# The context's output projection between the sample halves, the second matrix's sums two pairs late, and the spatial weights' low parts on VectorE

## The chip, the cores and the metric

The kernel runs on one core of one Trainium2 chip. The metric is device time in microseconds (us) for one execution. A core has TensorE (PE, matrix products; PEld is its weight loading), VectorE (DVE), ScalarE (ACT), GpSimd (POOL), and SyncE (SP), which here only issues DMAs. POOL and ACT issue DMAs too.

## The reference, cut

One layer of a diffusion backbone, applied to 1024 sample tokens and 256 context tokens (all float32, D = 1024, D_FF = 4096), with the same weights for both:

```
u   = rmsnorm(x, g1) * (1 + sc1) + sh1
xp, su, sv, q, k, v, o, gates, br = split(u @ w_in)
y_a = pool_branch(xp);  y_b = su * (w_sgu rmsnorm(sv) + b);  y_c = mlstm_branch(q, k, v, ...)
merged = sum_r sigmoid(br_r) * (y_r @ w_branch[r])
x   = x + gt1 * (merged @ w_out)                                  # output projection
u2  = rmsnorm(x, g2) * (1 + sc2) + sh2                            # modulation
x   = x + gt2 * (square(relu(u2 @ w_ff1)) @ w_ff2)                # feed-forward: first, second matrix
y   = rmsnorm(x, g_final)
```

The final states of the mLSTM for the context are outputs too.

## The kernel before

The 1280 rows are eight sample tiles of 128 rows (0 to 7, in groups 0 and 1 of 512 columns of the transposed data) and two context tiles (8 and 9, group 2). Every float32 product is made of three products of rounded parts: each operand is split into a high part (a cast, mostly on ACT) and a low part (raw minus high, mostly on DVE), and PE computes high x high, high x low, low x high. So every weight that is loaded costs a DMA, a cast and a subtraction ahead of PE. In the spatial projection (`sv`) the subtraction is on POOL (`eng=G`).

The stages by time: input, modulation and first projections to about 150 us; the mLSTM heads and the spatial values to 360; pooling and gating to 490; the gate products to 850; branch outputs to 1000; the output projection from about 1025; the feed-forward's first matrix from 1137 to 1549; its second matrix to the end.

The output projection `project_out(tiles, c0, n, weights)` makes `n` columns from `c0` on for each tile: 24 matmuls, then DVE multiplies by the gate and adds to the rows in `xt`, and ACT squares them for the norm (L1221 to L1224). Sample tiles take two halves of 512 columns, context tiles four quarters of 256 (`context_out(q)`, with weights of its own from `context_weights(q)`). `modulate_ff(g)` makes the norm of a group, the normalised rows (`xn`, half on ACT at L1184, half on DVE at L1186), transposes them on PE (`pt`, L1192), scales on ACT (L1201) and splits them.

The matrices of the feed-forward are multiplied by a scheme with seven products for a 2 x 2 block product (Strassen's, in Winograd's form), which needs sums of quarters. `quarter_sums` and `split_sum` (L824, L834) make T1 to T4 from the modulated rows. The first matrix is done in 16 pairs (`FeedPair`, fp 0 to 15) of 24.9 us: `begin` loads and splits raw weights (`a_..`, `s_..`), `contexts` does the context (`fc`), `rest` the products `fB` (with a quarter itself) and `fT` (with a sum), and `sums` makes from the four results, after relu and square, the second matrix's left operands: the results go to DRAM (`scr_h`, from ACT's queue), four sums on DVE (L1277 to L1280) go to `scr_s`, from POOL's queue. `second_sums(fp)` loads four quarters of the second matrix, has POOL make four differences in place (L1292) and stores them to `scr_t` (L1293).

The second matrix takes seven products in the order 1, 2, 6, 7, 4, 5, 3. For each of 16 fp a right operand (`r_`, from w_ff2 or `scr_t`) and a left one (`l_`, from `scr_h` or `scr_s`) is loaded by SP and split (L1352, L1353). PE multiplies them into the banks `w_0` to `w_3` (samples, 12 matmuls per fp); the context's rows (`c_`) go into `w_4`.

One SBUF buffer `z` holds 20 slots of 512 columns that are reused (`zs(i)`). In the feed-forward slots 0 to 3 and 4 to 7 hold raw weights of even and odd pairs, 12 to 15 and 8 to 11 the results of even and odd pairs, 16 to 19 the second matrix's quarters. The raw operands of the first ten fp of product 1 go into slots `FREE[fp]` and `FREE[fp] + 1`.

The order of instructions on each engine is set by a scheduler, which builds a timeline from the program's order and the free rooms. Where an engine is wrapped in `Pinned`, its instructions stay in the order in which the program writes them. An engine works through its queue in order, and so do the queues from which it issues DMAs.

Of the kernel before, what the change touches and what calls it, by code (L numbers as in the profile page):

```python
# [7 lines left out]
F32 = mybir.dt.float32  # L8
F32R = mybir.dt.float32r
AF = mybir.ActivationFunctionType  # L10
ALU = mybir.AluOpType
# [37 lines left out]
def hybrid_step(  # L49
# [39 lines left out]
    def load_w(src, name, raw=None, eng=V):  # L89
        raw = fetch_w(src, name) if raw is None else raw  # L90
        hi = wp.tile([P, 1024], F32R, tag="hi", name=f"hi_{name}", bufs=NHL)
        lo = wp.tile([P, 1024], F32R, tag="lo", name=f"lo_{name}", bufs=NHL)
        A.copy(hi, raw)
        eng.tensor_tensor(lo, raw, hi.bitcast(F32), ALU.subtract)
        return hi, lo
# [613 lines left out]
    vn = []  # L709
    vsq = cp.tile([P, NT, 2], F32, name="vsq")  # L710
    for q in range(2):
        wq = [load_w(w_sv[q, hf], f"sv{q}_{hf}", eng=G) for hf in range(2)]
        for i in range(NT):
            g, o = (i * P) // 512, (i * P) % 512
            if q == 0:
                vn.append(slot(f"vn{i}", F32))
            ps = ps_mm(f"sv{q}_{i}")
            for k in range(KT):
                whi, wlo = wq[k // 4]
                s = slice((k % 4) * 256, (k % 4 + 1) * 256)  # L720
                uh, ul = uT[k][g]
                PE.matmul(ps[:, :256], uh[:, o : o + P], whi[:, s], start=k == 0, stop=False)
                PE.matmul(ps[:, :256], ul[:, o : o + P], whi[:, s], start=False, stop=False)
                PE.matmul(ps[:, :256], uh[:, o : o + P], wlo[:, s], start=False, stop=k == KT - 1)
            A.copy(vn[i][:, q * 256 : (q + 1) * 256], ps[:, :256])
            A.activation(ps[:, 256:512], ps[:, :256], AF.Square, accum_out=vsq[:, i, q : q + 1])
# [6 lines left out]
    def zs(i, n=1):  # L733
        return z[:, i * 512 : (i + n) * 512]
# [185 lines left out]
    def load_half(src, name, view=lambda t: t):  # L920

        raw = first4(f"raw_{name}", F32)
        SP.dma_start(view(raw), src)
        hi, lo = six(f"hi_{name}"), ring(f"lo_{name}")
        A.copy(hi, raw)  # L925
        V.tensor_tensor(lo, raw, hi.bitcast(F32), ALU.subtract)
        return hi, lo
# [193 lines left out]
    def out_weights(hf, ks=range(KT)):  # L1121

        ws = []
        for k in ks:
            raw = tmp2(f"raw_wo{hf}_{k}")
            SP.dma_start(raw, w_out[hf, k])
            if hf == 0:
                rooms = (six, ring) if k < 6 else (first4, first4)
            else:
                rooms = (slot, slot) if k < 4 else (six, ring)  # L1130
            hi, lo = (room(f"{x}_wo{hf}_{k}") for room, x in zip(rooms, ("hi", "lo")))
            A.copy(hi, raw)
            V.tensor_tensor(lo, raw, hi.bitcast(F32), ALU.subtract)
            ws.append((hi, lo))
        return ws

    def context_weights(q):

        src = w_out[q // 2][:, :, q % 2 * 256 : q % 2 * 256 + 256].rearrange("(j k) p c -> j p k c", k=2)
        return [load_half(src[i], f"wc{q}_{i}", lambda t: t.rearrange("p (k c) -> p k c", k=2)) for i in range(4)]  # L1140

    w_out0 = out_weights(0)
    mT = [[] for _ in range(KT)]
# [24 lines left out]
    def modulate_ff(g):  # L1168
        t0, n = GROUPS[g]
        tiles = range(t0 // P, (t0 + n) // P)  # L1170
        fs = small([P, 4], f"fs{g}")[:, : len(tiles)]
        V.reduce_sum(fs, fsq[:, tiles[0] : tiles[-1] + 1, 0 : 4 if g == 2 else 2], axis=mybir.AxisListType.X)
        r = rstd_of(fs, len(tiles), f"f{g}")

        j = 1 if g == 2 else 0
        for qt in range(4):
            xn = []
            for ii, i in enumerate(tiles):
                if ii % 2 == 0:
                    t = tmp2(f"xn{i}_{qt}")  # L1180
                v = t[:, (ii % 2) * 256 : (ii % 2) * 256 + 256]
                xv = xt[i][:, qt * 256 : (qt + 1) * 256]
                if ii % 2 == 0:
                    A.activation(v, xv, AF.Copy, scale=r[:, ii : ii + 1])  # L1184
                else:
                    V.tensor_scalar(v, xv, r[:, ii : ii + 1], None, ALU.mult)  # L1186
                xn.append(v)
            for kk in range(2):
                k = qt * 2 + kk
                ps = ps_sd(f"pt2{g}_{k}")  # L1190
                for ii in range(n // P):
                    PE.transpose(ps[:, ii * P : (ii + 1) * P], xn[ii][:, kk * P : (kk + 1) * P], ident)  # L1192
                if g == 2:
                    c = slot(f"u2{k}c")
                    u2c[k] = hi, lo = c[:, 0:256], c[:, 256:512]
                    A.activation(ps[:, :n], ps[:, :n], AF.Identity, bias=sh2[:, k, j : j + 1], scale=a2[:, k, j : j + 1])
                    V.tensor_copy(hi, ps[:, :n])
                    V.tensor_tensor(lo, ps[:, :n], hi.bitcast(F32), ALU.subtract)
                    continue
                rf = raw2[g][k] = slot(f"u2r{k}_{g}", F32)  # L1200
                A.activation(rf, ps[:, :n], AF.Identity, bias=sh2[:, k, j : j + 1], scale=a2[:, k, j : j + 1])  # L1201
                if g == 0 or k >= 4:
                    hi, lo = slot(f"u2h{k}_{g}"), slot(f"u2l{k}_{g}")
                    V.tensor_copy(hi, rf)
                    V.tensor_tensor(lo, rf, hi.bitcast(F32), ALU.subtract)
                    u2s[f"B{1 + k // 4}{1 + g}", k % 4] = hi, lo

    def project_out(tiles, c0, n, weights):

        for i in tiles:  # L1210
            g = min(i // 4, 2)
            o = i * P - GROUPS[g][0]
            full = ps_mm(f"po{c0}_{i}")
            ps = full[:, :n]
            for k in range(KT):
                whi, wlo = weights(k)
                mh, ml = mT[k][g]
                PE.matmul(ps, mh[:, o : o + P], whi, start=k == 0, stop=False)
                PE.matmul(ps, ml[:, o : o + P], whi, start=False, stop=False)
                PE.matmul(ps, mh[:, o : o + P], wlo, start=False, stop=k == KT - 1)  # L1220
            V.tensor_tensor(ps, ps, gt1[(2 if g == 2 else 0) + c0 // 512][:, c0 % 512 : c0 % 512 + n], ALU.mult)  # L1221
            xc = xt[i][:, c0 : c0 + n]
            V.tensor_tensor(xc, xc, ps, ALU.add)  # L1223
            A.activation(ps, xc, AF.Square, accum_out=fsq[:, i, c0 // n : c0 // n + 1])  # L1224
            if c0 + n == D:
                SP.dma_start(scr_x[i], xt[i])

    def context_out(q):
        ws = context_weights(q)
        project_out((8, 9), q * 256, 256, lambda k: tuple(w[:, k % 2 * 256 : k % 2 * 256 + 256] for w in ws[k // 2]))  # L1230

    project_out(range(8), 0, 512, lambda k: w_out0[k])
    w_out1 = out_weights(1)
    project_out(range(5), 512, 512, lambda k: w_out1[k])
    modulate_ff(0)
    project_out(range(5, 8), 512, 512, lambda k: w_out1[k])
    context_out(0)
    context_out(1)  # L1240
    modulate_ff(1)
    quarters = (("B11", 0, 0), ("B21", 0, 4), ("B12", 1, 0), ("B22", 1, 4))
    raw2q = {nm: raw2[g][o : o + 4] for nm, g, o in quarters}
    context_out(2)
    context_out(3)

# [35 lines left out]

    def second_sums(fp):

        q = [zs(16 + i) for i in range(4)]
        for r in range(2):
            SP.dma_start(zs(16 + 2 * r, 2), w_ff2[2 * fp + r])
        b11, b12, b21, b22 = q  # L1290
        for out, x, y in ((b11, b12, b11), (b12, b22, b12), (b22, b22, b11), (b21, b22, b21)):
            G.tensor_tensor(out, x, y, ALU.subtract)  # L1292
        G.dma_start(scr_t[fp], zs(16, 4).rearrange("p (q c) -> p q c", c=512))  # L1293


    pairs = {}
# [1 line left out]
    def feed_pair(fp):  # L1298
        odd = fp % 2
        pairs[fp] = FeedPair(  # L1300
            f"{fp}", fp, (w_ff1[2 * fp], w_ff1[2 * fp + 1]), 4 if odd else 0, range(8, 12) if odd else range(12, 16), u2s, u2c)

    for fp in (0, 1):
        feed_pair(fp)
        pairs[fp].begin()
    modulate_ff(2)
    quarter_sums(raw2q)
    for nm in ("T4", "T3", "T2", "T1"):
        split_sum(u2s, raw2q, nm)
    for fp in (0, 1):  # L1310
        pairs[fp].contexts()
    for fp in range(NFP):
        if fp not in pairs:
            feed_pair(fp)
            pairs[fp].begin()
            pairs[fp].contexts()
        pairs[fp].rest()
        pairs[fp].sums()
        del pairs[fp]
        second_sums(fp)  # L1320


    pa.close()
# [21 lines left out]
    }  # L1345


    FREE = (0, 2, 16, 18, 12, 14, 4, 6, 8, 10)

    def split2(raw, room):  # L1350
        hi, lo = room("h"), room("l")
# [234 lines left out]
```

## Time and profile before

| | |
|---|---|
| median of 3 runs | 1937.88 us (1936.84 to 1939.31) |
| profiled execution | 1941.46 us |
| its span on the core | 1939.7 us |
| PE busy | 1905.1 us (98%) |
| DVE, ACT, POOL busy | 67%, 44%, 20% of the span |
| DMA | 318.56 MB, 164 GB/s over the span |

Times in the views are of the profiled execution, from the start of its span. A row of the timeline reads: start, duration, engine, line, operation, output<-inputs, shapes, count, and in brackets the idle time ahead of it with what ended it. A row of the waits reads: engine and what it waited with, what released it, us in all, times, longest. A row of DMA issues ends with the count, the size of one and the median time from issue to landing.

### The profile page before, as it was taken

The numbers are of one execution on the slowest core, as the hardware profiler recorded it, in microseconds if no ns is written. First come the engines' busy times: TensorE is split into PE (matmuls) and PEld (weight loads), VectorE is DVE, ScalarE is ACT, GpSimd is POOL, SyncE is SP. The second block draws the span as 40 slices with busy tenths as digits, with TensorE's granted clock in tenths as the row PEclk, the third lists the DMA queues.
The fourth block names the chain that finished last, engine by engine and source line by source line (L and its number), as shares of the span: only waits on it lengthen the run. The fifth ranks groups of instructions, "written<-read, shape, count | busy, mean of one in ns | idle before, by whom it ended". The sixth has DMA issues, their size and how long they took to land.

```text
span 1939.7 us, 28224 instructions
## 1 busy us (share of the span) xinstructions
PE 1905.1 (98%) x10142; PEld 1627.9 (84%) x10142; DVE 1305.4 (67%) x2234; ACT 849.2 (44%) x1771; POOL 378.3 (20%) x381
## 2 busy tenths in 40 slices
PE   8999999999999999999999999999999999999998
PEld 5888888988888888888888887888888888888886
DVE  6575344578697879866665599877876655644665
ACT  6444366632433333343123374444454545443443
POOL 1100011063032422220000015544431210000003
PEclk9999999999999999999999999999999999999999
DMA  9211111125453444379623426667774686655544
GB/s 368 79 60 38 40 39 42 43 84 187 141 170 138 147 137 157 127 241 329 201 66 121 161 94 243 248 241 271 248 251 141 207 317 201 211 171 151 163 135 160
DMA packets 152774, 318.56 MB, mean 164 GB/s; under 512 B 17934, under 2 KB 42226, under 8 KB 150586
## 3 DMA queue, kind: packets, MB, share of 16 engines
q1 hardware_dynamic: 109082, 223.35, 34.9%
q0 software_dynamic: 15520, 57.75, 8.1%
q10 hardware_dynamic: 28032, 35.67, 5.2%
q8 instruction: 79, 1.29, 0.3%
q14 instruction: 61, 0.50, 0.1%
HBM read 220.21 MB, written 95.98 MB: 163 GB/s over the span
## 4 chain that ended last, share of the span: by engine, by line
PE 86%; DVE 5%; DMA 4%; ACT 2%; POOL 2%; issue 1%; SPq 0%; POOLq 0%; ACTq 0%; DVEq 0%
PE w L1453 6%; PE w L1455 6%; PE w L1454 6%; PE pb L1100 3%; PE pb L1101 3%; PE pb L1102 3%; PE fT_g L934 3%; PE fT_g L935 3%; PE fT_g L936 3%; PE fT L936 2%; PE fT L934 2%; PE fT L935 2%; PE fB_g L936 2%; PE fB_g L934 2%; PE fB_g L935 2%; PE fB L936 2%
## 5 line engine op out<-in xcount | busy, mean ns | idle before, releaser
L1292 POOL TENSOR_TENSOR z<-z 128x512 f32<-128x512 f32 x64 | 100.4, 1568 | 124.3 <-DMA z<-in_w_ff 121.3
L579 POOL PARTITION_ALL_REDUCE acc<-acc x16 | 55.1, 3479 | 224.9 <-DVE acc L573 141.5
L991 DVE TENSOR_TENSOR z<-z 128x512 f32<-128x512 f32 x120 | 95.2, 793 | 2.7
L573 DVE SCALAR_TENSOR_TENSOR acc<-z,scond,acc 128x512 f32<-128x512 f32 x112 | 82.2, 780 | 0.0
L1407 POOL TENSOR_TENSOR rs_y<-rs_y,neghalf 128x1 f32<-128x1 f32 x10 | 9.5, 956 | 333.7 <-DVE rs_y L1406 333.7
L1258 ACT ACTIVATE z<-z 128x512 f32<-128x512 f32 x64 | 40.4, 632 | 74.7 <-DVE z L1000 40.4
L1017 ACT ACTIVATE z<-z 128x512 f32<-128x512 f32 x56 | 35.4, 632 | 60.7 <-DVE z L1000 16.0
L130 POOL TENSOR_TENSOR rs_h<-rs_h,neghalf 128x4 f32<-128x4 f32 (+1 forms) x12 | 10.9, 910 | 171.6 <-DVE rs_h L129 137.8
L1106 DVE TENSOR_TENSOR sg<-pb,sg 128x512 f32<-128x512 f32 (+1 forms) x48 | 28.7, 599 | 23.3 <-PE pb L1102 23.2
L1259 ACT ACTIVATE z<-z 128x512 f32<-128x512 f32 x64 | 40.2, 629 | 1.1
L1221 DVE TENSOR_TENSOR po<-po,gt 128x512 f32<-128x512 f32 (+1 forms) x24 | 14.6, 607 | 35.6 <-PE po L1220 35.5
L925 ACT CAST hi_wb<-raw_wb 128x512 fp32r<-128x512 f32 x24 | 14.8, 620 | 53.2 <-PE pb L1101 42.9
L782 POOL TENSOR_TENSOR z<-z 128x256 f32<-128x256 f32 (+13 forms) x20 | 34.7, 1746 | 13.7 <-ACT z L767 5.5
L1283 POOL DMA_DIRECT2D scr_s<-x x48 | 26.3, 549 | 54.6 <-DVE x L1277 49.0
L624 DVE SCALAR_TENSOR_TENSOR z<-z,dmb,kv 128x129 f32<-128x129 f32 x56 | 17.1, 346 | 27.4 <-PE kv L613 27.2
L580 POOL TENSOR_TENSOR acc<-acc,bt 1x512 f32<-1x512 f32 x16 | 23.4, 1475 | 60.0 <-issue 60.0
L1224 ACT ACTIVATE po<-z 128x512 f32<-128x512 f32 (+1 forms) x24 | 12.7, 529 | 48.6 <-DVE z L1223 34.3
L1107 DVE TENSOR_TENSOR z<-z,sg 128x512 f32<-128x512 f32 (+1 forms) x48 | 28.6, 600 | 1.1
L681 DVE TENSOR_TENSOR den<-den,gcol 128x2 f32<-128x2 f32 x40 | 6.0, 158 | 34.2 <-ACT den L680 34.0
L606 DVE TENSOR_TENSOR z<-tv,gcol 128x512 f32<-128x512 f32 (+1 forms) x24 | 14.1, 601 | 18.6 <-ACT z L603 18.3
L650 DVE SCALAR_TENSOR_TENSOR w<-rb,gcol,cst 128x128 f32<-128x128 f32 x48 | 13.3, 343 | 19.4 <-PE rb L646 19.4
L1000 DVE TENSOR_TENSOR z<-z 128x512 f32<-128x512 f32 x30 | 26.3, 877 | 0.0
(5360 smaller groups left out, 7269.0 us busy)
## 6 DMA issues: line engine op xcount, KB each, us to landing
z<-in_w_ff SPq DMA_DIRECT2D x64, 512.0 KB, 5.6
z<-in_w_ada SPq DMA_DIRECT2D x64, 256.0 KB, 3.1
scr_t<-z POOLq DMA_DIRECT2D x16, 1024.0 KB, 4.4
z<-in_w_in SPq DMA_DIRECT2D x28, 512.0 KB, 4.4
scr_g<-z ACTq DMA_DIRECT2D x48, 256.0 KB, 2.0
sg<-scr_g SPq DMA_DIRECT2D x48, 256.0 KB, 4.7
scr_h<-z ACTq DMA_DIRECT2D x48, 256.0 KB, 3.7
scr_s<-x POOLq DMA_DIRECT2D x48, 256.0 KB, 4.4
```

What stands on the lines that cost most here:

```text
L573: V.scalar_tensor_tensor(acc[j], raw, scond[:, k, j : j + 1], acc[j], ALU.mult, ALU.add)
L934: PE.matmul(ps, whi[:, s], ahi, start=first and k == ks[0], stop=False)
L935: PE.matmul(ps, whi[:, s], alo, start=False, stop=False)
L936: PE.matmul(ps, wlo[:, s], ahi, start=False, stop=end and k == ks[-1])
L991: V.tensor_tensor(out, x, y, op)
L1100: PE.matmul(pb[:, :n], whi[:, s], yh, start=kc == 0, stop=False)
L1101: PE.matmul(pb[:, :n], whi[:, s], yl, start=False, stop=False)
L1102: PE.matmul(pb[:, :n], wlo[:, s], yh, start=False, stop=kc == 3)
L1292: G.tensor_tensor(out, x, y, ALU.subtract)
L1453: PE.matmul(banks[j], h_[:, s], rh, start=fp == 0, stop=False)
L1454: PE.matmul(banks[j], l_[:, s], rh, start=False, stop=False)
L1455: PE.matmul(banks[j], h_[:, s], rl, start=False, stop=fp == NFP - 1)
```

## The change

1. The low parts of the spatial projection's weights (four subtractions of 128 x 1024) move from POOL to DVE.
2. The context's output projection, all four quarters, moves to between the two sample halves, and its weights get other rooms. `modulate_ff(2)` (context) comes after tile 3 of the second half, `modulate_ff(0)` after tile 4, `modulate_ff(1)` at the end. The context products of the first two pairs come ahead of the quarter sums.
3. The results of pairs move to slots 16, 17, 12, 13 (even) and 18, 19, 8, 9 (odd), so the first pairs' results stand where the raw rows of the gate stage were; the second matrix's quarters move to slots 10, 11, 14, 15. `FREE` changes with them.
4. The second matrix's sums of pairs 0 to 5 are written out up to two pairs late (`LATE`), and POOL is pinned in the loop over pairs, so that each pair's sums come behind its own `scr_s` stores. `scr_t` is stored in two DMAs of 512 KB instead of one of 1 MB.

```
-        wq = [load_w(w_sv[q, hf], f"sv{q}_{hf}", eng=G) for hf in range(2)]
+        wq = [load_w(w_sv[q, hf], f"sv{q}_{hf}") for hf in range(2)]
...
     project_out(range(8), 0, 512, lambda k: w_out0[k])
+    for q in range(4):
+        context_out(q)
     w_out1 = out_weights(1)
-    project_out(range(5), 512, 512, lambda k: w_out1[k])
+    project_out(range(4), 512, 512, lambda k: w_out1[k])
+    modulate_ff(2)
+    project_out((4,), 512, 512, lambda k: w_out1[k])
     modulate_ff(0)
     project_out(range(5, 8), 512, 512, lambda k: w_out1[k])
-    context_out(0)
-    context_out(1)
     modulate_ff(1)
...
-    context_out(2)
-    context_out(3)
...
-        q = [zs(16 + i) for i in range(4)]
+        q = [zs(i) for i in (10, 11, 14, 15)]
         for r in range(2):
-            SP.dma_start(zs(16 + 2 * r, 2), w_ff2[2 * fp + r])
+            SP.dma_start(zs(10 + 4 * r, 2), w_ff2[2 * fp + r])
...
-        G.dma_start(scr_t[fp], zs(16, 4).rearrange("p (q c) -> p q c", c=512))
+        for r in range(2):
+            G.dma_start(scr_t[fp][:, 2 * r : 2 * r + 2, :], zs(10 + 4 * r, 2).rearrange("p (q c) -> p q c", c=512))
...
-            f"{fp}", fp, (w_ff1[2 * fp], w_ff1[2 * fp + 1]), 4 if odd else 0, range(8, 12) if odd else range(12, 16), u2s, u2c)
+            f"{fp}", fp, (w_ff1[2 * fp], w_ff1[2 * fp + 1]), 4 if odd else 0, (18, 19, 8, 9) if odd else (16, 17, 12, 13), u2s, u2c)
     for fp in (0, 1):
         feed_pair(fp)
         pairs[fp].begin()
-    modulate_ff(2)
+    for fp in (0, 1):
+        pairs[fp].contexts()
     quarter_sums(raw2q)
     for nm in ("T4", "T3", "T2", "T1"):
         split_sum(u2s, raw2q, nm)
-    for fp in (0, 1):
-        pairs[fp].contexts()
+    G = Pinned(tc, nc.gpsimd)
+    LATE = {0: (), 1: (), 2: (0,), 3: (1, 2), 4: (3,), 5: (4, 5)}
     for fp in range(NFP):
...
         pairs[fp].sums()
         del pairs[fp]
-        second_sums(fp)
+        for late in LATE.get(fp, (fp,)):
+            second_sums(late)
+    G = nc.gpsimd
...
-    FREE = (0, 2, 16, 18, 12, 14, 4, 6, 8, 10)
+    FREE = (0, 2, 10, 14, 16, 12, 4, 6, 18, 8)
```

POOL at the end of the first matrix, before: the stores of pair 15's sums (`scr_s15`) and then the reloads of the rows (`scr_x`). The differences of all 16 pairs stand further up in the queue.

```order
L1281 DMA scr_c13_10963<-xc_15_14788 512x1x128
L1482 DMA z_76<-scr_x8_9893 128x1024
...
L1337 DMA gf1_14830<-in_gfin 128x512
L1283 DMA scr_s15_10979<-x1_15_14785 128x512
L1283 DMA scr_s15_10979<-x2_15_14786 128x512
L1283 DMA scr_s15_10979<-z_76 128x512
L1283 DMA scr_s15_10979<-x4_15_14787 128x512
L1482 DMA z_76<-scr_x9_9894 128x1024
```

The same place after (L43 is the line of `Pinned` that issues):

```order
L43 DMA scr_s15_11052<-x1_15_14800 128x512
L43 DMA scr_s15_11052<-x2_15_14801 128x512
L43 DMA scr_s15_11052<-z_76 128x512
L43 DMA scr_s15_11052<-x4_15_14802 128x512
L43 TENSOR_TENSOR z_76<-z_76 128x512 x4
L43 DMA scr_t15_11068<-z_76 128x1024 x2
L1496 DMA z_76<-scr_x5_9890 128x1024
```

The four differences of pair 15 and their two stores now stand behind the stores of its sums.

PE in product 1 of the second matrix, before, the first use of `r1_2` (right operand of fp 2), ahead of the context's bank `w1_4`:

```order
L1453 MATMUL w1_3_14846<-r1_1h_14871,l1_1h_14876 128x512
L1454 MATMUL w1_3_14846<-r1_1h_14871,l1_1l_14877 128x512
L1455 MATMUL w1_3_14846<-r1_1l_14872,l1_1h_14876 128x512
L1453 MATMUL w1_0_14843<-r1_2h_14893,l1_2h_14898 128x512
L1454 MATMUL w1_0_14843<-r1_2h_14893,l1_2l_14899 128x512
```

And after:

```order
L1467 MATMUL w1_4_14863<-r1_0h_14865,c1_0h_14954 128x512
L1468 MATMUL w1_4_14863<-r1_0h_14865,c1_0l_14955 128x512
L1469 MATMUL w1_4_14863<-r1_0l_14866,c1_0h_14954 128x512
L1467 MATMUL w1_4_14863<-r1_1h_14887,c1_0h_14954 128x512
L1468 MATMUL w1_4_14863<-r1_1h_14887,c1_0l_14955 128x512
L1469 MATMUL w1_4_14863<-r1_1l_14888,c1_0h_14954 128x512
L1467 MATMUL w1_4_14863<-r1_2h_14909,c1_0h_14954 128x512
L1468 MATMUL w1_4_14863<-r1_2h_14909,c1_0l_14955 128x512
L1467 MATMUL w1_0_14859<-r1_2h_14909,l1_2h_14914 128x512
```

Six matmuls of the context with fp 0 and 1 now stand between the sample rows of fp 1 and the first use of fp 2.

PE between the output projection and the feed-forward, before (`po768` is the context's last quarter, `fB11_0` the first product of pair 0):

```order
L1218 MATMUL po768_9_10911<-hi_wc3_3_10878,m7c_9865 128x256
L1219 MATMUL po768_9_10911<-hi_wc3_3_10878,m7c_9865 128x256
L1220 MATMUL po768_9_10911<-lo_wc3_3_10879,m7c_9865 128x256
L934 MATMUL fB11_0_11002<-u2h0_0_10331,a11_0h_10998 128x512
L935 MATMUL fB11_0_11002<-u2l0_0_10332,a11_0h_10998 128x512
```

And after (`po512_7` is tile 7's second half, `fc0` the context product of pair 0, whose first row is shown; `pt21` are the transposes of group 1):

```order
L1229 MATMUL po512_7_10883<-lo_wo1_7_10487,m7h1_9840 128x512
L934 MATMUL fc0_11151<-u20c_10617,a11_0h_11071 128x256
...
L936 MATMUL fc1_11213<-u27c_10675,a12_1l_11132 128x256
L1201 MATMUL pt21_0_10923<-cst_78,xn4_0_10917 128x128 x2
...
L1201 MATMUL pt21_7_11002<-cst_78,xn6_3_10988 128x128 x2
L934 MATMUL fB11_0_11075<-u2h0_0_10726,a11_0h_11071 128x512
```

The context's projection no longer stands ahead of the feed-forward; the context products of pairs 0 and 1 and the transposes of group 1 do.

More of the change, by code (lines that the diff above doesn't have):

```diff
@@ L1139, in context_weights @@
         src = w_out[q // 2][:, :, q % 2 * 256 : q % 2 * 256 + 256].rearrange("(j k) p c -> j p k c", k=2)
-        return [load_half(src[i], f"wc{q}_{i}", lambda t: t.rearrange("p (k c) -> p k c", k=2)) for i in range(4)]
+        rooms = (six, ring) if q % 2 else (slot, slot)
+        ws = []
+        for i in range(4):
+            raw = tmp2(f"raw_wc{q}_{i}")
+            SP.dma_start(raw.rearrange("p (k c) -> p k c", k=2), src[i])
+            hi, lo = (room(f"{x}_wc{q}_{i}") for room, x in zip(rooms, ("hi", "lo")))
+            A.copy(hi, raw)
+            V.tensor_tensor(lo, raw, hi.bitcast(F32), ALU.subtract)
+            ws.append((hi, lo))
+        return ws
     w_out0 = out_weights(0)
```

## The prediction

> **What bounds the kernel now.** I read the page's busy table first, then the chain of work that ended last, then windows over the stages that the change touches.
>
> ```profile
> PE 1905.1 (98%) x10142; PEld 1627.9 (84%) x10142; DVE 1305.4 (67%) x2234; ACT 849.2 (44%) x1771; POOL 378.3 (20%) x381
> PE 86%; DVE 5%; DMA 4%; ACT 2%; POOL 2%; issue 1%; SPq 0%; POOLq 0%; ACTq 0%; DVEq 0%
> ```
>
> TensorE (PE) is busy 98% of the span of 1939.7 us, so only two things can move the time: stretches in which PE idles now, and new ones. No matmul is added or taken away. The windows show where PE idles around the change (columns: length, then busy us and count for PE, PEld, DVE, ACT, POOL, then granted clock, DMA share, GB/s):
>
> ```profile
> 1000.00:1050.00 50.00, 50.00 (x239) 42.07 (x238) 31.41 (x56) 16.47 (x37) 4.24 (x8) 1.00 0.35 116
> 1050.00:1100.00 50.00, 50.00 (x237) 41.69 (x235) 22.68 (x42) 15.97 (x37) 1.06 (x1) 1.00 0.33 119
> 1100.00:1150.00 50.00, 46.97 (x318) 43.12 (x316) 44.59 (x93) 34.38 (x72) 2.22 (x2) 1.00 0.35 119
> 1150.00:1200.00 50.00, 47.74 (x249) 40.28 (x250) 47.14 (x74) 27.78 (x56) 28.08 (x18) 0.97 0.51 179
> 1200.00:1250.00 50.00, 48.38 (x261) 41.04 (x260) 39.42 (x59) 26.38 (x50) 21.89 (x25) 1.00 0.78 279
> 1400.00:1450.00 50.00, 48.21 (x255) 41.35 (x254) 35.87 (x57) 25.96 (x50) 17.85 (x20) 1.00 0.82 274
> 1550.00:1600.00 50.00, 49.45 (x217) 40.46 (x218) 26.84 (x43) 22.35 (x42) 5.89 (x11) 1.00 0.90 321
> 1850.00:1900.00 50.00, 50.00 (x222) 41.39 (x222) 36.74 (x63) 21.25 (x39) 4.57 (x3) 1.00 0.43 133
> ```
>
> PE idles 3.0 + 2.3 + 1.6 = 6.9 us at the start of the feed-forward (1100 to 1250), where VectorE (DVE) is near full; 1.8 us after 1400; 0.6 us after 1550, where the second matrix begins. The longest wait at the start is 3.0 us for ScalarE's normalised rows, and after it the granted clock drops:
>
> ```profile
> PE pt L1192 <- ACT xn L1184: 3.0, 1, 3.0
> 1148.00:1152.00 4.00, 2.03 (x10) 1.92 (x10) 1.90 (x7) 3.56 (x9) 0.70 (x1) 0.76 0.45 139
> 1152.00:1156.00 4.00, 3.92 (x28) 3.61 (x27) 3.98 (x12) 2.92 (x7) 0.34 (x1) 0.81 0.65 254
> ```
>
> The shortfall is (0.24 + 0.19) x 4 = 1.7 us at most: the price I use for the slow clock after any idle time of 3 us or more. So the start costs 6.9 + 1.7 = 8.6 us.
>
> **The end of the feed-forward: a new wait.** This is the term that decides. Product 1 of the second matrix loads its operands into z slots by FREE. Before, fp 2 used slots 16 and 17, the old room of the second matrix's sums, whose last occupant left at pair 10. After, fp 2 and 3 use slots 10, 11, 14, 15, the new room, and the order on POOL puts the sums of pair 15 behind that pair's four scr_s stores, which are among the last things the feed-forward makes. SP's load of r_2 (and l_2, and all that is queued behind them on SP) waits for scr_t of pair 15 to land. PE has r_0 and r_1 to work on: 24 matmuls for the sample rows and 6 for the context, then it needs r_2. The rows of before that price the chain:
>
> ```profile
> 1548.93 0.39 PE L1453 MATMUL w<-r_0h,l_0h 128*128 128x512 f32 x1
> 1549.13 0.69 DVE L1007 TENSOR_TENSOR z<-z,fB 128x512 f32<-128x512 f32 x1 [1.44 <-PE fB L936]
> 1548.39 0.63 ACT L1259 ACTIVATE z<-z 128x512 f32<-128x512 f32 x1
> 1555.28 0.68 DVE L1279 TENSOR_TENSOR z<-z 128x512 f32<-128x512 f32 x1
> 1555.88 0.68 DVE L1280 TENSOR_TENSOR x<-z,x 128x512 f32<-128x512 f32 x1
> 1556.85 0.54 POOL L1283 DMA_DIRECT2D scr_s<-x  x1
> 1407.29 5.38 POOL L1292 TENSOR_TENSOR z<-z 128x512 f32<-128x512 f32 x4 [8.01 <-DMA z<-in_w_ff]
> 1425.67 4.68 POOL L1292 TENSOR_TENSOR z<-z 128x512 f32<-128x512 f32 x3 [0.49 <-DMA z<-in_w_ff]
> 1412.96 0.57 POOL L1293 DMA_DIRECT2D scr_t<-z  x1 [0.30 <-POOL z L1292]
> 1183.51 4.24 DMA scr_t<-z
> 1549.44 0.61 ACT L1352 CAST r_4h<-z 128x512 fp32r<-128x512 f32 x1
> sg<-scr_g SPq DMA_DIRECT2D x48, 256.0 KB, 4.7
> z<-in_w_ada SPq DMA_DIRECT2D x64, 256.0 KB, 3.1
> z<-in_w_ff SPq DMA_DIRECT2D x3, 256.0 KB, 8.0
> scr_s<-x POOLq DMA_DIRECT2D x3, 256.0 KB, 8.4
> ```
>
> (The last two are of the window 1540 to 1580.) On before's clock, with the last product of pair 15 read out from 1549.1:
>
> - readout 0.69, relu and square 2 x 0.63: 1551.1. The four sums follow each other by 0.60 (1555.28 to 1555.88), so 3 x 0.60 + 0.68: 1553.6. After's order has no casts of r_3 to r_7 between them as before has; they wait behind r_2.
> - the last scr_s issue 0.54: 1554.1. POOL's four subtractions 5.38: 1559.5 (the row with three of them gives 6.2 for four). A gap of 0.30 and the first scr_t issue 0.57: 1560.4.
> - scr_t lands 4.24 later (that row is for 1 MB; here half a MB is enough, but the other half follows at once): 1564.6.
> - r_2 is loaded: 4.7, the median of a 256 KB load in the run. The rows' ends are 3.1 and 8.0; the 8.0 belongs to a stretch with the DMA engines 90% busy (window 1550), and here SP's queue stands still, so I take the middle row, nearer the low end. 1569.3. Cast to r_2's high part 0.61: 1569.9.
> - PE is ready for it at 1548.9 + 30 x 0.225 (50.00 us / 222, window 1850) = 1555.7.
>
> Wait: 14.2 us. With the slow clock after it 15.9, less the 0.6 that this window idles already: **+15.3**. Low end: 3.1 for the load, half of the slow clock's price, 1 us less for scr_t: 12. High end: 6.2 for the subtractions, 8.4 for scr_t as scr_s took in that window, 8.0 for the load: 22.5 + 1.7 = 24. Nothing covers it: SP, PE and both element-wise engines stand behind the same load. The reloads of xt (POOL, behind scr_t in its queue) are used only when product 2 is read out, some 87 us after product 1 begins (2 x 192 matmuls x 0.225), so their delay costs nothing.
>
> On DMA times the Trainium skill states a rule ("DMA: Bandwidth & Descriptors", section "Anatomy of one DMA — SWDGE (gpsimd) path"): about 2.0 us fixed plus bytes over 436 GB/s. By it 512 KB and 256 KB would take an estimated 3.2 and 2.6 us where I put 4.24 and 4.7; the term would be about 12.2 instead of 15.3 and the forecast about 1945.4. The rows above are longer than the rule at every size, so the sum keeps the rows.
>
> **The start of the feed-forward.** The context's projection (its weights on SP, casts on ACT, subtractions on DVE, 8 read-outs) moves to 1068 and on, beside windows in which DVE has 19 and 27 of 50 us free and ACT 34; its weights now use tmp2 and other rooms, and their loads come ahead of out_weights(1) on SP, where the DMA engines are a third busy. I cost it at nothing; without the cover it would be 14 casts and 14 subtractions too late, at most the 3 us that PE waits at the start now. What the end of projection now is: tile 7, then modulate_ff(1). What PE may do until T4 (first product that needs quarter sums) is complete: 48 context matmuls of pair 0 and 48 of pair 1 at about half a 512-wide one (0.12), 48 of product B11 (0.225), 16 transposes of group 1 in 4 steps, and three quarters of T4's first block: 11.5 + 10.8 + 4 + 2 = 28. What DVE has to do until T4's last low part, counted in after's order from the normalised rows: 16 quarter sums, 4 high and 4 low parts of group 1, 4 + 4 low parts of t2 and T4, and the pair's own splits and sums: 49 instructions, 35 of them at 0.60, 4 casts, 4 small ones and 6 sums of z.
>
> ```profile
> 1144.64 0.68 DVE L824 TENSOR_TENSOR u2r<-u2r,u2r 128x512 f32<-128x512 f32 x1
> 1145.24 0.68 DVE L834 TENSOR_TENSOR t2l<-u2r,t2h 128x512 fp32r<-128x512 f32 x1
> L130 POOL TENSOR_TENSOR rs_f<-rs_f,neghalf 128x4 f32<-128x4 f32 x2 | 2.6, 1290 | 83.8 <-DVE rs_f L129 83.8
> 1157.09 1.80 DVE L834 TENSOR_TENSOR T4l<-u2r,T4h 128x512 fp32r<-128x512 f32 x1
> ```
>
> The first two give the step of 0.60. 35 x 0.60 + 14 at about 0.45 is 27.5; ahead of it stand two read-out operations (1.3), the square (0.8), the power on POOL (1.3) and eight normalised blocks (about 3): 34 to 35. Idle time: 6.5, plus 1.7 of slow clock if one piece is 3 us, about 8.2 against 8.6. What does go is the contention: 1157.09 is a subtraction of 1.80 that runs beside POOL's subtractions, against 0.68 alone, and pair 0's second sums now come two pairs later, so this and the later gaps to 1250 (1.6) should shrink. I take **-2**; ends -8.6 (all of the loss goes) and +3 (a second wait as long as the one of now).
>
> **The gap after 1400.**
>
> ```profile
> ACT a_11h L916 <- DMA z<-in_w_ff: 6.4, 1, 6.4
> PE fc L934 <- ACT hc L1262: 1.8, 1, 1.8
> ```
>
> Pair 11's first weights land late and PE loses 1.8 with them. In after's order on SP the raw weights of pair n+2 stand ahead of the sums' loads of pair n, or between the two, from pair 1 on, so they aren't queued behind a wait for the sums' room: **-1.8**; ends 0 and -2.2. The same order is why I cost the pinned POOL queue in the middle pairs at nothing: the sums' four subtractions and stores take some 10 us of a pair's 25.
>
> **Spatial weights on VectorE.** Four subtractions move from POOL to DVE, beside the mLSTM heads.
>
> ```profile
> L94 POOL TENSOR_TENSOR lo_sv<-raw_sv,hi_sv x4: 2369/2392/2412, 223.5 to 313.6; 128x1024 fp32r<-128x1024 f32 x4
> PE th L690 <- ACT z L689: 5.0, 2, 3.6
> ```
>
> They take 2.4 us each on POOL. On DVE four of them are at most 9.6 us in 90, and PE's waits there are for ACT's rows of the heads, a chain in which lo_sv does not stand. A subtraction ahead of a step of that chain could delay it by up to 2.4: **0**, ends -1.5 and +2.4.
>
> **Sum.** 15.3 - 2 - 1.8 + 0 = +11.5. The profiled execution took 1941.46 and would take 1953; it lies 3.6 above the median of 1937.88, so the median is forecast at **1949**. A change within 0.2%, 3.9 us, can't be told from none.
>
> **Rivals.**
> - *The wait is there but short, and the start recovers* (0.14). Wait at its floor of 12, start at -8.6, gap -1.8: 1939.5, no measurable change. For it: the DMA is light when SP stands still. Against it: DVE's 34 us at the start are counted, not guessed.
> - *No wait at the second matrix* (0.11). If r_2's load does not depend on pair 15's stores in time, for example because POOL works through the sums while PE still has pair 15's last products, nothing is left but -2, -1.8 and the 0.6: 1933.5, faster. It decides once what is left of the wait is below 4.4 - 3.9 = 0.5 us, or below 11 - 3.9 = 7 us if the whole 8.6 at the start goes too. Against it: the chain from the last read-out to a cast r_2 is 19 us even with the low ends, PE's cover 6.8.
> - *Longer still* (0.15). The wait at its high end, 24, or a second wait at the start, +3: 1937.9 + 24 - 1.8, about 1960. For it: the window 1550 to 1600 has the DMA engines 90% busy now, and scr_s took 8.4 there.
>
> My forecast has 0.60. Faster 0.11, same 0.15, slower 0.74. The range from 1938 to 1958 leaves out the case without a wait and the upper part of the longer one.
>
> **What would show it.** In the profile after: PE idle in one piece of 12 to 20 us, some 7 us after the first matmul of the second matrix, released by r_2's cast, and the granted clock low behind it; on POOL four subtractions and two scr_t issues after pair 15's scr_s; r_2's load issued just after scr_t lands. The start: PE waiting at group 1's transposes and at T4 for 5 to 8 us in all, DVE full, no subtraction of 1.8 before pair 2. After 1400 no wait for weights. The heads as before within 2 us. The forecast is wrong if POOL's stores of pair 15 come well before PE's last matmul of that pair, or if the start, which has the least certain term, turns out to lose nothing.

## The result and the profile after

The changed kernel is slower: 1959.13 us (median of 4 runs, 1955.55 to 1960.67) against 1937.36 (1935.97 to 1939.31), a ratio of 1.0109 (95% interval 1.0091 to 1.0127), about +21.8 us. The forecast was 1949, in a range of 1938 to 1958: the sign was right, the size half of what came, and the time lies just above the range. The two profiled executions, 1941.46 and 1958.53, are 17.1 apart; that of before lay 4 us above its median, so the accounts below, which are of these two, come to less than the medians do.

The busy table first. PE has the same 10142 matmuls; what grew is its idle time (span less busy time), from 34.6 to 50.0 us.

```profile
PE 1906.7 (97%) x10142; PEld 1629.2 (83%) x10142; DVE 1309.8 (67%) x2238; ACT 851.3 (44%) x1771; POOL 366.6 (19%) x393
```

The same windows as before the change, and those around the end of the first matrix (columns as in the prediction):

```profile
1100.00:1150.00 50.00, 49.48 (x283) 42.24 (x282) 37.90 (x85) 30.90 (x64) 2.02 (x2) 1.00 0.34 127
1150.00:1200.00 50.00, 47.05 (x227) 38.02 (x227) 46.92 (x83) 32.18 (x58) 5.31 (x9) 1.00 0.36 122
1200.00:1250.00 50.00, 50.00 (x268) 43.30 (x268) 33.34 (x57) 24.45 (x46) 12.40 (x18) 1.00 0.50 183
1400.00:1450.00 50.00, 50.00 (x267) 43.28 (x266) 39.24 (x55) 26.11 (x50) 20.42 (x24) 1.00 0.63 227
1500.00:1550.00 50.00, 46.06 (x236) 38.91 (x234) 33.14 (x48) 21.58 (x40) 22.68 (x30) 1.00 0.81 276
1550.00:1600.00 50.00, 30.59 (x116) 24.12 (x117) 25.32 (x37) 20.45 (x37) 9.96 (x14) 0.73 0.85 301
```

Before the change, the window from 1500 to 1550 was:

```profile
1500.00:1550.00 50.00, 49.90 (x263) 42.74 (x262) 33.57 (x58) 27.57 (x52) 10.64 (x19) 1.00 0.58 192
```

The start of the feed-forward (first three rows) idles 3.5 us where it idled 6.9, and its clock stays at 1.00; the gap after 1400 is gone. But between 1500 and 1600 PE idles 23.3 us, against 0.7 before, and the clock is 0.73 in the second of these windows. Counted from its first matmul, the second matrix begins at 1540.69, 8.2 us earlier than before (1548.93), and takes 416.0 us to the end of the span where it took 390.8: 25.2 more. PE's waits between 1530 and 1600 name the cause (engine and what waited, what released it, us in all, times, longest):

```profile
PE w L1467 <- ACT r_2h L1366: 18.0, 1, 18.0
PE w L1467 <- ACT c_0h L1366: 4.0, 1, 4.0
PE w L1468 <- DVE c_0l L1367: 1.1, 1, 1.1
```

The 18.0 are the wait that was forecast, for r_2 in the room of the second matrix's sums. The 5.1 ahead of it are for the context's left operand c_0, which was not forecast; it cost little by itself, since PE would have reached r_2 by so much sooner and waited there.

What made the chain long stands in the order of time on the engines and on SP's queue (timeline of after; start, duration, engine, what), and in the DMA issues from 1540 to 1576:

```profile
1540.89 0.69 DVE L1007 TENSOR_TENSOR z<-z,fB 128x512 f32<-128x512 f32 x1 [1.43 <-PE fB L936]
1544.88 0.69 DVE L1289 TENSOR_TENSOR x<-z,x 128x512 f32<-128x512 f32 x1
1548.30 0.54 POOL L43 DMA_DIRECT2D scr_s<-x  x1 [0.85 <-DMA gt<-scr_mod]
1548.85 5.99 POOL L43 TENSOR_TENSOR z<-z 128x512 f32<-128x512 f32 x4
1554.79 1.09 POOL L43 DMA_DIRECT2D scr_t<-z  x2
1563.38 0.56 SPq L1375 DMA_DIRECT2D z<-in_w_ff  x1
1571.90 0.62 ACT L1366 CAST r_2h<-z 128x512 fp32r<-128x512 f32 x1 [5.78 <-DMA z<-in_w_ff]
1572.57 0.79 PE L1467 MATMUL w<-r_2h,c_0h 128*128 128x512 f32 x1 [17.99 <-ACT r_2h L1366]
scr_t<-z POOLq DMA_DIRECT2D x2, 512.0 KB, 7.5
z<-in_w_ff SPq DMA_DIRECT2D x4, 256.0 KB, 8.5
1560.00:1565.00 5.00, 0.00 (x0) 0.00 (x0) 0.00 (x0) 0.00 (x0) 0.00 (x0) 0.50 1.05 380
```

The order is the one forecast: read-out, sums, stores of the sums, subtractions, scr_t, r_2. But from 1554.8, where POOL issues scr_t, to 1571.9 the engines wait for DMAs; all they do is to cast and subtract two operands of the context. In the window 1560 to 1565 no engine has done anything, while the DMA engines are full (1.05) and move 380 GB/s: besides scr_t they carry loads that SP had issued ahead of r_2, for later fp and for the next product.

One link differs from the forecast. r_2 goes into the slots of the first scr_t store, and that store had landed at 1561.6, 6.8 us after its issue at 1554.79. r_2's load was issued only at 1563.38. The chain of work that ended last shows what SP waited for (start, duration, what):

```profile
1543.38 12.15 DMA l_10r<-scr_h
1555.59 7.72 DMA l_13r<-scr_h
1563.38 8.50 DMA z<-in_w_ff
```

SP issued l_13r when l_10r had landed, and r_2 when l_13r had landed. So the last 1.8 us ahead of r_2's issue are SP's own queue and not scr_t.

### The profile page after: what moved, and what is told of

It is laid out like the page before. It is cut to its first block, busy times and chain, and to the rows that moved or that the text cites. A ratio compares the mean times of both kernels' runs of the same rounds, so it can differ in the third digit from the quotient of the medians.

```text
span 1956.7 us, 28251 instructions
## 1 busy us (share of the span) xinstructions
PE 1906.7 (97%) x10142; PEld 1629.2 (83%) x10142; DVE 1309.8 (67%) x2238; ACT 851.3 (44%) x1771; POOL 366.6 (19%) x393
## 4 chain that ended last, share of the span: by engine, by line
PE 93%; DMA 3%; ACT 1%; DVE 1%; issue 1%; POOL 0%; SPq 0%; ACTq 0%; POOLq 0%; DVEq 0%
PE w L1467 6%; PE w L1468 6%; PE w L1469 6%; PE fT L934 3%; PE fT L936 3%; PE fT L935 3%; PE pb L1100 3%; PE pb L1101 3%; PE pb L1102 3%; PE fT_g L936 2%; PE fT_g L934 2%; PE fT_g L935 2%; PE fB L934 2%; PE fB L935 2%; PE fB L936 2%; PE po L1228 2%
## 5 line engine op out<-in xcount | busy, mean ns | idle before, releaser
L43 POOL TENSOR_TENSOR z<-z 128x512 f32<-128x512 f32 x64 | 91.2, 1425 | 42.8 <-DMA z<-in_w_ff 39.4
L991 DVE TENSOR_TENSOR z<-z 128x512 f32<-128x512 f32 x120 | 89.0, 742 | 2.7
L43 POOL DMA_DIRECT2D scr_s<-x x48 | 26.6, 555 | 127.5 <-DVE x L1286 112.3
L43 POOL DMA_DIRECT2D scr_c<-xc x16 | 11.7, 734 | 84.4 <-DVE xc L1289 78.3
L1000 DVE TENSOR_TENSOR z<-z 128x512 f32<-128x512 f32 x30 | 24.2, 805 | 0.0
```

Of the source, the lines that this page charges most:

```text
L43: return self.tc.keep_in_program_order(getattr(self.eng, op)(*args, **kw))
L991: V.tensor_tensor(out, x, y, op)
```

## The experiments

Each ran beside the kernel before on the same chip; ratios are to that (its medians there were 1939.0 to 1939.6), with their 95% intervals.

**Other slots for product 1.** `free6`:

```
-    FREE = (0, 2, 10, 14, 16, 12, 4, 6, 18, 8)
+    FREE = (0, 2, 16, 12, 4, 6)
```

> The changed kernel with FREE = (0, 2, 16, 12, 4, 6): product 1's operands of fp 2 and 3 no longer go into the room of the second matrix's sums, and from fp 6 on they go into small rotating rooms; nothing else differs. Theory A (the loss is the wait for slots that the sums of pair 15 still hold): the profile after shows 18.0 + 4.0 + 1.1 us of waits at the second matrix and a clock of 0.5 behind them, 28 us less the 2.4 that before lost there; all of it goes, 1931 to 1934 us. Theory B (the DMA engines are full there, so whatever comes third is late, in any slot): r_2 lands 8 us or more after its issue again, and c_0 is waited for 4 us: 1940 to 1950 us.

Measured 1935.72 us, 0.9986 (0.9978 to 0.9995): by the ratios 24 us less than the changed kernel, from one line of slots. It takes product 1's operands out of the sums' room, and it also sends those from fp 6 on into rotating rooms; `free4` below keeps the sums' room with such rotating rooms and stays slow, so the sums' room is what counts. No wait for r_2 is left. What is left of theory B is the wait for c_0 alone:

```profile
PE w L1467 <- ACT c_0h L1366: 2.7, 1, 2.7
```

**The sums one pair early, same slots.** `sums_one_early`:

```
-    LATE = {0: (), 1: (), 2: (0,), 3: (1, 2), 4: (3,), 5: (4, 5)}
+    LATE = {0: (), 1: (), 2: (0,), 3: (1, 2), 4: (3,), 5: (4, 5), 13: (13, 14), 14: (15,), 15: ()}
```

> The changed kernel with its own FREE, but the second matrix's sums of pair 14 written with pair 13, those of pair 15 with pair 14, so the room is free some 20 us before the second matrix begins. Theory A: the wait goes as with the other slots, 1931 to 1936 us. Theory B: the room was not the cause, 1945 us or more. If only this one is fast and the other slots are not, it was the order on POOL's queue (reloads of the rows behind the sums) and not the room.

Measured 1947.28 us, 1.0042 (1.0029 to 1.0054): the number that theory B allowed, which `free6` contradicts, and a miss for theory A as it stood. Pair 15's sums stand ahead of its stores here, and still r_2 is waited for:

```profile
PE w L1467 <- ACT r_2h L1366: 9.8, 1, 9.8
1529.85 10.40 DMA z<-in_w_ff
1544.38 5.85 DMA scr_t<-z
1550.67 9.80 DMA z<-scr_h
```

The last three are of the chain of work that ended last: the sums' own load took 10.4 us, their store 5.85, and the load of l_2 behind it 9.8. So being written early is not enough; the sums' transfers stand in the full stretch themselves. Together with `free6` this gives the cause two halves: the room decides that there is a wait, and the landing times with full DMA engines how long it is.

**Fewer loads ahead of r_2.** `free4`, with FREE = (0, 2, 10, 14):

> The changed kernel with FREE = (0, 2, 10, 14): fp 2 and 3 still wait for the room of pair 15's sums, but operands from fp 4 on go into small rotating rooms, so fewer loads stand ahead of r_2 on SP and in the DMA engines. If my prediction's step failed by the load of the DMA engines alone (scr_t landed in 7.5 us where I put 4.2, r_2 in 8.5 where I put 4.7), both land sooner here, in 4 to 6 us, and the wait is 13 to 17 us instead of 23: 1948 to 1954 us. If the times do not depend on the loads ahead, 1959 us.

Measured 1958.71 us, 1.0100 (1.0086 to 1.0114): no gain, against what I expected. The chain of work that ended last tells why:

```profile
1546.06 11.90 DMA z<-in_w_ff
1561.98 6.95 DMA scr_t<-z
1568.98 3.61 DMA z<-in_w_ff
```

r_2's load took 3.61 us here where it took 8.5, so that link is short when little stands ahead of it, as I had thought. But the second half of pair 15's quarters, now issued later, took 11.9 and held the subtractions back. The delay moved along the chain; the DMA engines were no emptier (340 GB/s from 1540 to 1576, 326 in the changed kernel). In this run scr_t is what r_2's load waited for.

**All sums ahead of the full stretch.** `catch_up`, in the rooms and with the FREE of the changed kernel:

```
+    LATE = {0: (), 1: (), 2: (0,), 3: (1, 2), 4: (3,), 5: (4, 5), 6: (6, 7), 7: (8,), 8: (9, 10), 9: (11,), 10: (12, 13), 11: (14,), 12: (15,), 13: (), 14: (), 15: ()}
```

> The changed kernel with its rooms, FREE and order, but the second matrix's sums catch up: pairs 6 to 15 are written one or two per pair, and pair 15's stand behind pair 12. The room is free some 60 us before the second matrix, and no sums stand in its DMA stretch. Theory A+B (the wait is the room's, and its length is the full DMA engines'): with sums one pair early r_2 was still waited for 9.8 us, because the loads and stores of those sums took 6 to 10 us each in that stretch; with all of them ahead of it no wait is left, 1929 to 1934 us. If the DMA engines are full there without the sums too, and that alone makes the wait, 1940 to 1948 us.

Measured 1933.59 us, 0.9966 (0.9953 to 0.9978), the lowest ratio of the study. Around the start of the second matrix PE idles 0.55 us, like the kernel before:

```profile
1500.00:1550.00 50.00, 50.00 (x263) 43.13 (x263) 34.52 (x60) 29.22 (x56) 10.65 (x19) 1.00 0.77 251
1550.00:1600.00 50.00, 49.45 (x218) 40.47 (x217) 27.23 (x44) 21.79 (x39) 5.96 (x11) 1.00 0.88 313
```

The DMA engines are as full (0.88 against 0.85), but PE waits neither for r_2 nor for c_0: nothing that it needs soon depends on a chain through them. A gap at pair 11 came back (`PE fc` waits 1.5 us).

**The same, more evenly.** `catch_spread` writes sums 7 and 8 behind pair 7, 12 and 13 behind pair 11, 15 behind pair 13, and one pair's behind each between.

> The changed kernel with the second matrix's sums catching up one pair later and more evenly: 7 and 8 behind pair 7, 12 and 13 behind pair 11, 14 behind 12, 15 behind 13. With the first catching-up order PE lost 1.7 us at pair 11, whose weights came late as in the kernel before. If that gap is made by two pairs' sums behind pairs 8 and 10, it goes: 1930 to 1933 us, where the first order gave 1933.6. If pair 15's sums at pair 13 come too near the full stretch, r_2 is waited for again, 1935 us or more.

Measured 1933.70 us, 0.9970 (0.9960 to 0.9979). The gap at pair 11 is gone from the profile (PE 50.00 of 50 from 1400 to 1450); the time can't be told from `catch_up`.

**The first pairs' sums on time.** `no_late`, with `LATE = {}`:

> The changed kernel with LATE empty: the second matrix's sums of each pair, the first ones too, are written right behind the pair, POOL still pinned. The end is as in the changed kernel (wait of 23 us). What it tells is what the lateness of the first pairs is worth at the start: if the first sums' loads and subtractions are what made the context's move alone slow (there the weights of pair 2 came 8 us late), this is 4 to 10 us slower than the changed kernel, 1963 to 1969 us; if the rooms or the pinned queue are enough, 1959 us.

Measured 1958.41 us, 1.0097 (1.0083 to 1.0110), as the changed kernel; PE's waits at the start are the same (2.7 us for T4). So the lateness of the first pairs, taken by itself, is worth nothing: with POOL pinned, pair 0's sums stand behind its stores anyway, past the crowded part of the start.

**The context's move alone.** `part_context` is the kernel before with part 2 of the change.

> The kernel before with part 2 alone (the context's output projection between the halves, its weights' rooms, the order of the modulations and of the first context products). Theory A: no wait at the second matrix, the start of the feed-forward loses 3 to 5 us less than before, with the second sums of the first pairs still beside it: 1932 to 1936 us. Theory C: 1945 us or more, with a wait at the second matrix.

Measured 1954.22 us, 1.0075 (1.0063 to 1.0088). Both theories failed: it is slow, but not at the second matrix. PE idles 17.3 us from 1100 to 1250, against 6.9 before, and its waits are there:

```profile
PE fc L934 <- ACT a_2h L916: 7.8, 1, 7.8
1141.17 1.27 POOL L1301 TENSOR_TENSOR z<-z 128x512 f32<-128x512 f32 x1 [9.52 <-DMA z<-in_w_ff]
1162.84 4.13 DMA scr_t<-z
1171.08 16.37 POOL z L1301
1192.82 4.26 DMA scr_t<-z
1197.99 5.12 DMA z<-in_w_ff
```

The scheduler, free to order POOL, puts the sums of the first pairs into the time that the context left. There a subtraction of POOL, 1.27 us at 1141 with VectorE nearly idle, took 16.37 beside VectorE's unbroken row of instructions; the store came after it, SP held the next loads for that room, and behind these stood pair 2's weights.

**POOL not pinned.** `nopin` is the changed kernel without `G = Pinned(tc, nc.gpsimd)` in the loop.

> The changed kernel without the pinned POOL queue; the order in which the sums are written stays. The scheduler then puts the sums far ahead (those of pairs 0 to 3 before pair 0's own stores, pair 15's beside pair 8). Theory: no wait for r_2 at the end, but the start is as in the part with the context alone: POOL's subtractions stretch beside VectorE's full queue, the loads for them hold SP, and pair 2's weights come late: 1945 to 1955 us. If the start was slow there for another reason (the rooms of the results), this one is 1930 to 1935 us.

Measured 1953.36 us, 1.0073 (1.0059 to 1.0087), as the theory had it. No wait for r_2, and the start's loss is back:

```profile
1166.99 19.22 POOL L1301 TENSOR_TENSOR z<-z 128x512 f32<-128x512 f32 x3 [4.28 <-DMA z<-in_w_ff]
PE fc L934 <- ACT a_1h L916: 5.6, 1, 5.6
```

So the pinned queue is what makes the context's move pay at the start, and what puts pair 15's sums in the way at the end.

**The other parts alone.** `part_late` is the kernel before with parts 3 and 4. The context's rows are still in slots 16 to 19 there when the first pairs' results are written, so the context's output is of overwritten rows; the instructions are the same.

> The kernel before with parts 3 and 4 alone (rooms, late sums, pinned POOL, FREE); context and spatial weights as before. Theory A: the whole wait at the second matrix is here, about +26, and the start loses what it lost before or a little more, since the first pair's results wait for the context's rows: 1960 to 1968 us. Theory C (the wait comes from the order that the context's move gives to the loads): 1935 to 1945 us.

Measured 1959.18 us, 1.0101 (1.0085 to 1.0116): the wait is there without the context's move (14.4 us for r_2, 5.4 for c_0), somewhat shorter than expected, and theory C falls.

**The spatial weights alone.** `part_sv` is the kernel before with part 1.

> The kernel before with part 1 alone (the spatial weights' four low parts on VectorE). Prediction: nothing, within 1.5 us of before (1936 to 1939). If VectorE's four instructions of 2 us lie in the heads' chain: up to 2.4 us slower.

Measured 1937.22 us, 0.9984 (0.9975 to 0.9993). That is about 3 us faster (1.4 to 4.8 by the interval), by its middle more than the 1.5 I allowed. Its profile shows the heads' waits almost as before (L690 4.7 in all, 5.0 before); where the 3 us come from I can't say.

**Part 2 with POOL pinned and all sums early.** `ctx_pin_catch` leaves out parts 1 and 3: it keeps the rooms and the FREE of before.

> The kernel before with part 2 (context between the halves), POOL pinned and the catching-up order of the sums, but with the rooms and FREE of before and the spatial weights' low parts on POOL. If the order of the sums is all that matters, this is as fast as the changed kernel with the catching-up order, 1931 to 1936 us. If part 3 (results where the gate's rows were, other rooms for the sums) is needed for the start, pair 0 waits for rooms there and it is 1938 us or more.

Measured 1939.37 us, 0.9994 (0.9981 to 1.0006). By its median this is the second case, 1938 or more, but the wait for rooms that was to explain it is not there: its runs scatter from 1933 to 1944, and its profiled execution, with a span of 1932.5, shows no wait of any size that the faster kernels lack. Whether the rooms of part 3 are worth something by themselves stays open.

## Why the prediction was right in sign and wrong in size

- *The wait at the second matrix: the mechanism was right in the main, the term mis-sized.* Forecast were +15.3: 14.2 of wait and 1.7 of slow clock, less 0.6. The second matrix took 25.2 longer: 23.1 of waits, and a clock of 0.50 from 1550.5 to 1577.8, in which the 12 matmuls after the wait took about 0.43 us each instead of 0.23, some 2.5 us. Taken link by link, in us after pair 15's last read-out began:

| link | forecast | measured |
|---|---|---|
| the four sums ready | 4.5 | 4.7 |
| last scr_s issued | 5.0 | 8.0 |
| subtractions done | 10.4 | 14.0 |
| scr_t's first half landed | 15.5 | 20.7 |
| r_2 issued | 15.5 | 22.5 |
| r_2 landed | 20.2 | 31.0 |

  The engines' work was right within 0.6. Of the 10.8 that were missing, 3.0 arose up to the last scr_s, nearly all of it waits ahead of POOL's stores, which the prediction put at nothing (the last two stores were released by earlier loads of POOL's own queue, as in the row at 1548.30); 0.6 are the subtractions, 1.6 scr_t's landing, 1.8 SP's queue, and 3.8 r_2's landing. The step that failed is the choice of the load's price, "here SP's queue stands still, so I take the middle row", and with it 4.24 for scr_t, a row of a stretch with the DMA engines half busy. SP's queue did not stand still: from 1538.8 to 1562.4 it issued 19 loads that the scheduler had put ahead of r_2. They filled the DMA engines, and at the end they held r_2's issue itself. So the sign "r_2's load issued just after scr_t lands" was met only within 1.8 us, and another landing set the moment. The rows with prices near what was measured, 8.0 and 8.4 us from the very window, stood in the prediction as the high end; with them for both transfers the term is 15.3 + 4.2 + 3.3 = 22.8, and the forecast 1957. That sum would in part be luck: its 8.4 for scr_t stands for 6.8 of landing and 1.8 of SP's queue.
- *The Trainium skill's rule on DMA times* ("DMA: Bandwidth & Descriptors", section "Anatomy of one DMA — SWDGE (gpsimd) path") would have put the term at 12, further off still: its figure is that of one transfer, and none of those that mattered had the engines to itself (6.8 and 8.1 us for the two 512 KB of scr_t, 8.5 for the 256 KB of r_2). The Trainium skill gives it for DMAs that POOL issues; r_2's load is SP's. Two things in the prediction's paragraph on it are wrong: with a term of 12.2 its sum is 1946.3 and not 1945.4, and the rows are not longer than that rule at every size, since the 1 MB of the row at 1183.51 took 4.24 where the rule gives an estimated 4.4.
- *The start: right sign, too small.* Forecast -2; measured 3.5 us idle instead of 6.9 and no slow clock (1.7 before), -5.1. PE's longest wait there is 1.4 us:

```profile
PE fT L934 <- ACT T4h L833: 2.7, 2, 1.4
```

  T4 is the last thing to come, as forecast, and DVE was nearly full (46.92 of 50 us from 1150 to 1200). I gave the contention with POOL too little: POOL did no subtraction from 1100 to 1200, where before it did twelve, and `part_context` and `nopin`, which put them back, lose more than before. The trace of before had shown more of it than the 1.80 I quoted:

```profile
1169.88 13.33 POOL L1292 TENSOR_TENSOR z<-z 128x512 f32<-128x512 f32 x4 [7.22 <-DMA z<-in_w_ff]
```

- *The gap after 1400* went as forecast (-1.8). In all, PE reached the second matrix 8.2 us earlier, against -3.8 forecast. Besides the start and the gap, about 1.5 of it stand ahead of the output projection, where nothing was forecast.
- *Spatial weights*: forecast 0, ends -1.5 and +2.4; measured about -3 alone, outside these ends by its middle. The reason is open.
- *Rivals.* "Longer still" (0.15), with the wait at its high end, gave 1960 and is what happened: 24 against the 25.2 of the second matrix. That its sum lies so close to 1959.13 is partly luck, since it takes only 1.8 off for everything ahead of the second matrix, where the profiled executions show 8.2, and these are 17.1 apart where the medians are 21.8. The rival without a wait was priced 1933.5; `catch_up`, which takes the wait away and keeps the rest, came to 0.9966 of before, 1931.3 from the forecast's 1937.88.

## What to carry to other kernels

When a buffer is given a second use, follow its last tenant to the end of its stores, count what the scheduler has put ahead of the new load in its queue (19 loads here), and price each transfer in that chain by rows from the same stretch of time, not by the same transfer elsewhere: 256 KB took 3.6 us in `free4` and 8.5 in the changed kernel. Work that depends on nothing but a buffer (the second matrix's sums) should be done by the time the DMA engines fill, and what of it runs on POOL kept out of a stretch in which VectorE works without a break. A pinned queue removed one loss and made another; the change with one line of its table altered beats both kernels, 0.9966 (0.9953 to 0.9978) of the time before.

## What the runs showed of the hardware that I had not expected

POOL can be all but stopped by DVE. In `part_context` a subtraction of 128x512 took 1.27 us at 1141, where DVE did almost nothing, and 16.37 us from 1171.08 on, beside 26 DVE instructions of the same size that followed each other by 0.60. DVE's own slowed to 1.77 only at the end, when POOL got through:

```profile
1178.19 0.68 DVE L917 TENSOR_TENSOR s_0l<-z,s_0h 128x512 fp32r<-128x512 f32 x1
1187.91 1.77 DVE L917 TENSOR_TENSOR s_1l<-z,s_1h 128x512 fp32r<-128x512 f32 x1
```

The Trainium skill says that POOL shares a read and a write interface with DVE ("Advanced Engine Details and Errata", section "GPSIMD Details"); the trace agrees, and shows that the loss falls mostly on POOL.

The issue of a DMA can be held by an earlier DMA of the same queue: SP issued l_13r 0.06 us after l_10r had landed, and r_2 0.07 us after l_13r had. No run here shows what limits the number in flight.

The slow clock lasts after the wait: PE ran at 0.50 for 5 us after it resumed at 1572.6.
